# An encoder layer on one core: attention branch A's reciprocal row sums are transposed once and read back from DRAM spread over the channels, instead of being widened and transposed tile by tile

## The chip, the cores and the metric

The kernel runs on one core of a Trainium2 chip. The metric is the device time of one execution in microseconds (us); less is better. Before the change three runs gave 1674.7, 1675.51 and 1675.98 us.

Names of the engines in what follows: PE is TensorE (matmuls and transposes), DVE is VectorE, ACT is ScalarE, POOL is GpSimd, and SP is SyncE, which here only issues DMAs. Each engine works through its own instructions in order.

## The reference

One encoder layer (width 1024) is applied to two inputs: 1024 positions (the sample) and 256 positions (the prompt). The kernel works on both as one list of 1280 rows, 10 tiles of 128. Everything is float32.

```
h = rmsnorm(x, g_mix);  z = h @ w_in          # queries, keys, values of A and B, and gate logits
o_a = banded_attention(8 heads of 64, window 128, with a sink per head)     # branch A
o_b = dilated_mixture(3 groups x 4 heads of 64)                             # branch B
merged = sigmoid(gate_a) * (o_a @ w_branch_a) + sigmoid(gate_b) * (o_b @ w_branch_b)
x = x + merged @ w_out
y = rmsnorm(x + square(relu(rmsnorm(x, g_mlp) @ w_up)) @ w_down, g_final)
```

What matters here is the end of branch A's attention. For each position and head the kernel has the sum of the unnormalized values and the denominator; the output is their quotient:

```
denom = sum(p) + exp(sink - m)
o = (p @ v) / denom
```

## The kernel before, in words

A float32 product is made of three matmuls of a reduced type (fp32r): each operand is split into a high and a low part (`hi`, `lo`), high on ACT (a copy), low on DVE (a subtraction). `mm3` (line 188) emits them.

The stages that matter follow each other on PE. First comes **the attention of branch A** (lines 1430 to 1459): four units (two heads each) times ten tiles, with the last gate logits of `logits` (line 1223, the "fill") woven in between, 4 matmuls of 512 columns or 8 of 256 at a step. `exponential` (line 1177) leaves each row's sum in `l_a`, 128 positions x (8 heads x 10 tiles). `values_of` (line 1198) writes the unnormalized output, transposed, so that its partitions are the channels of two heads (64 each) and its columns the positions, to DRAM (`scr_o`). `sums_a` (line 1215) adds the sink's part and takes the reciprocal of `l_a`, in place, on DVE.

Then comes **the gate stage** (lines 1469 to 1540), 48 jobs. A job is one block of positions (512, 512 or 256), one branch, and one 128-wide group of the 1024 columns. A `b` job has 6 matmuls, an `a` job 12; the order is 8 `b` jobs of block 0, then 4 `a` jobs of block 0, then the same for blocks 1 and 2, then the remaining `a` jobs. Each job's result is multiplied on DVE by its gate `sg` (lines 1535 to 1538), which SP loads from DRAM six jobs ahead (`load_gate`, line 1473) and ACT turns into a sigmoid three jobs ahead (`open_gate`, line 1483). A job's matmuls go to one of the three PSUM banks of tag `mm`.

Beside those jobs the `a` operand is made (`side`, line 1504): `load_o` (line 1387) reads two tiles of `scr_o` back; `widen` (line 1394) copies, on POOL, `l_a`'s reciprocals of two tiles out to `wl`, 128 positions x (8 heads x 64), each value 64 times; `turn_a` (line 1400) transposes the four 128x128 squares of a tile's `wl` on PE into a PSUM bank, multiplies `o` with it on DVE (line 1409), and makes the high part on ACT (line 1415); `low_a` (line 1417) makes the low part on DVE. The first `a` job needs all of this for tiles 0 to 3. It also needs its weights, which `prepare` (line 224) splits: ACT at line 231, DVE at line 235.

What sets the order: up to `last.close()` (line 1503) the program's order is kept on every engine as written (`manual_schedule`). From there to line 1635, which holds the whole gate stage, a planner orders each engine's instructions, by the program's order as priority and by its own estimate of when each one's inputs and buffers are there. On the chip each engine then keeps that order, whether or not it has to wait. Tiles come from shared rings: `slot` hands out the 33 buffers of tag `m` (`sg`, `o`, `wl`, and the high and low parts), `wslot` the 10 of tag `w`.

Of the kernel before, what the change touches and what calls it, by code (L numbers as in the profile page):

```python
# [10 lines left out]
F32 = mybir.dt.float32  # L11
F32R = mybir.dt.float32r
AF = mybir.ActivationFunctionType
ALU = mybir.AluOpType

P = 128
# [3 lines left out]
T = NS + NP  # L20
NT = T // P
BLOCKS = ((0, 512), (512, 512), (1024, 256))
HD = 64
AH = 8
# [26 lines left out]
HALVES = (slice(0, HD), slice(HD, P))  # L51
# [46 lines left out]
def encoder_kernel(  # L98
# [5 lines left out]
    nc = tc.nc  # L104
# [16 lines left out]
    dram = ctx.enter_context(tc.tile_pool(name="dram", bufs=1, space=bass.MemoryType.DRAM))  # L121
# [5 lines left out]
    def slot(name, shape=(P, D), dt=F32):  # L127
        return slots.tile(list(shape), dt, name=name, tag="m", bufs=N_M)
# [7 lines left out]
    def bank(tag, name=None):  # L136
        return psum.tile([P, 512], F32, name=name or tag, tag=tag, bufs={"mm": 3, "sc": 2, "pt": 2, "pv": 1}[tag])
# [58 lines left out]
    def run(gen):  # L196
        for _ in gen:
            pass
# [47 lines left out]
    ident = const.tile([P, P], F32, name="ident")  # L246
# [4 lines left out]
    nsink = const.tile([P, AH], F32, name="nsink")  # L251
# [25 lines left out]
    scr_n = dram.tile([2, ROWS * P], F32, name="scr_n")  # L277
    scr_c = dram.tile([1, ROWS * P], F32, name="scr_c")
    scr_o = [dram.tile([P, 4, 2, P], F32, name=f"scr_o{t}") for t in range(0, NT, 2)]
    scr_x = [dram.tile([P, D], F32, name=f"scr_x{t}") for t in range(NT)]  # L280

    scr_u = [dram.tile([P, 7, 4, TH], F32, name=f"scr_u{g}") for g in range(FF // P // 8)]
# [383 lines left out]
    def load_h21():  # L666
        for i in range(2):
            h21[i] = slot("hhi", (P, 2, 512), F32R), slot("hlo", (P, 2, 512), F32R)
            for j in range(2):
                nc.sync.dma_start(h21[i][j].bitcast(F32), scr_h[i][:, j])  # L670
# [18 lines left out]
    with ExitStack() as pre:  # L689
# [200 lines left out]
        for t in range(2, NT):  # L890
# [13 lines left out]
            ps = bank("mm", "v")  # L904
# [20 lines left out]
        for t in (4, 5, 6, 7, 8, 9, 0, 1, 2, 3):  # L925
            ps = bank("mm", "v")
# [6 lines left out]
    if True:  # L933
# [188 lines left out]
        b, p = iter(()), parts0  # L1122
        att_b = iter(())
        for first, last, name in ((0, MIXED, "pairs"), (MIXED, len(PAIRS), "mixed")):
            with tc.tile_pool(name=name, bufs=1) as now[0]:
                if first:
                    att_b = attention_b(stage)
                for j in range(first, last):
# [4 lines left out]
                    b, p = pair(b, p, PAIRS[j], PAIRS[j + 1] if j + 1 < len(PAIRS) else None, hooks, tick, first)  # L1133
# [10 lines left out]
    if True:  # L1144
        att_pool = ExitStack()
        att = att_pool.enter_context(tc.tile_pool(name="att", bufs=3))
        nm_a, l_a = (att.tile([P, AH, NT], F32, name=x, tag=x, bufs=1) for x in ("nm_a", "l_a"))

        def a3(name, shape=(P, 2, 3 * P), n=3, dt=F32):
            return att.tile(list(shape), dt, name=name, tag=name, bufs=n)  # L1150
# [61 lines left out]
            nc.vector.tensor_copy(o, pv[:, : 2 * P].rearrange("p (i q) -> p i q", i=2))  # L1212
            nc.sync.dma_start(scr_o[t // 2][:, u], o)

        def sums_a():

            sinks = nsink.unsqueeze(2).to_broadcast([P, AH, NT])
            nc.vector.tensor_tensor(nm_a, nm_a, sinks, op=ALU.subtract)
            nc.scalar.activation(nm_a, nm_a, AF.Exp)
            nc.vector.tensor_tensor(l_a, l_a, nm_a, op=ALU.add)  # L1220
            nc.vector.reciprocal(l_a, l_a)

        def logits():

            for i, c in enumerate(PLAIN):
                hi, lo = weight(0)
                for t0, n in BLOCKS[::2] + BLOCKS[1:2]:
                    if i + 1 < len(PLAIN) and t0 == 0:
                        fetch()
                    ps = bank("mm")  # L1230
                    yield from mm3(ps[:, :n], [((hi[:, k, :], lo[:, k, :]), h_at(k, t0, n)) for k in range(KC)],
                                   4 if n == 512 else 8)
                    z = wslot("gs", (P, 512))
                    nc.scalar.activation(z[:, :n], ps[:, :n], AF.Copy)
                    nc.sync.dma_start(scr_g[c][:, t0 : t0 + n], z[:, :n])
                    if i + 1 < len(PLAIN) and t0 == NS:
                        prepare()
# [132 lines left out]
    if True:  # L1370
# [18 lines left out]
                rows_o[t] = slot("o", (P, 4, 2, P))  # L1389
                nc.sync.dma_start(rows_o[t], scr_o[t // 2])  # L1390

        wide_l = {}

        def widen(t):

            r = wide_l[t // 2] = slot("wl", (P, 2, AH, HD))
            for i in range(2):
                nc.gpsimd.tensor_copy(r[:, i], l_a[:, :, t + i].unsqueeze(2).to_broadcast([P, AH, HD]))

        def turn_a(t):  # L1400
            if t in (0, 4, 8):
                o_hi.block(t // 4)
                o_lo.block(t // 4)
            o = rows_o[t - t % 2][:, :, t % 2, :]
            ps = bank("pt")
            r = wide_l[t // 2][:, t % 2].rearrange("p h d -> p (h d)")
            for k in range(4):
                nc.tensor.transpose(ps[:, P * k : P * k + P], r[:, P * k : P * k + P], ident)
            nc.vector.tensor_tensor(o, o, ps.rearrange("p (k q) -> p k q", k=4), op=ALU.mult)
            per = o_hi.per(P * t)  # L1410
            parts = [(o_hi.at(k, P * t, P, per), o_lo.at(k, P * t, P, per), o[:, k : k + per, :])
                     for k in range(0, 4, per)]
            banks_t["a", t] = parts
            for hi, _, src in parts:
                nc.scalar.activation(hi, src, AF.Copy)

        def low_a(t):
            for hi, lo, src in banks_t.pop(("a", t)):
                nc.vector.tensor_tensor(lo, src, hi.bitcast(F32), op=ALU.subtract)

        load_h21()
        load_prompt(0, unit0[0])
# [2 lines left out]
        n = len(order)  # L1425
# [34 lines left out]
        prepare()  # L1460
        values_of(*order[n - 2])
        sums_a()
        run(merges)
        next(fill)
# [8 lines left out]
        def load_gate(i):  # L1473
            if i < len(jobs):
                x, b, c = jobs[i]
                t0, n = BLOCKS[b]
                if c % 2 == 0:
                    z = slot("sg", (P, 2, 512))
                sgs[i] = z[:, c % 2, :n] if c % 2 == 0 else sgs[i - 1, 0][:, 1, :n]
                sgs[i, 0] = z if c % 2 == 0 else None  # L1480
                nc.sync.dma_start(sgs[i], scr_g[c + KC * (x == "b")][:, t0 : t0 + n])

        def open_gate(i):
            if i < len(jobs):
                c = jobs[i][2] + KC * (jobs[i][0] == "b")
                nc.scalar.activation(sgs[i], sgs[i], AF.Sigmoid, bias=bg[:, c : c + 1])
# [5 lines left out]
        load_gate(3)  # L1492
        load_o(3)
        for i in range(4):
            if i < 2:
                widen(2 * i)
            if i < 3:
                open_gate(i)
            next(fill)
        run(fill)  # L1500
        load_gate(4)
        load_gate(5)
        last.close()
        side = {0: [(turn_a, 0)], 1: [(low_a, 0), (turn_a, 1)], 2: [(low_a, 1)],
                3: [(turn_a, 2), (widen, 4)], 4: [(low_a, 2), (turn_a, 3)], 5: [(low_a, 3)],
                6: [(high_b, 1)], 7: [(low_b, 1)],
                9: [(turn_a, 4), (widen, 6)], 10: [(low_a, 4), (turn_a, 5)], 11: [(low_a, 5)],
                13: [(turn_a, 6), (widen, 8)], 14: [(low_a, 6)], 15: [(turn_a, 7)], 16: [(low_a, 7)],
                17: [(high_b, 2)], 18: [(low_b, 2)],
                20: [(turn_a, 8)], 21: [(low_a, 8)], 22: [(turn_a, 9)], 23: [(low_a, 9)]}  # L1510
        for i, (x, b, c) in enumerate(jobs):
            t0, n = BLOCKS[b]
# [15 lines left out]
            ps = bank("mm")  # L1528
# [79 lines left out]
    with ExitStack() as pre:  # L1608
# [20 lines left out]
        for hh in range(2):  # L1629
# [17 lines left out]
            for t in range(NT):  # L1647
                m = parts.pop(t)
                ps = bank("mm")
# [393 lines left out]
```

## Time and profile before

| | before |
|---|---|
| runs shown, us | 1674.7, 1675.51, 1675.98 (median 1675.51) |
| span of the profiled execution, us | 1672.7 |
| median of the runs above that span, us | 2.8 |
| PE busy, us | 1661.8 (99%) |
| DVE / ACT / POOL busy, us | 951.1 / 714.3 / 494.3 |
| granted PE clock in the gate stage | 1.00 |
| HBM read / written, MB | 175.13 / 90.92 |

The span runs from the first to the last instruction that the profiler recorded. The times of the runs hold what lies around it; the page gives the profiled execution no other time of its own than the span. The two agree to within 2.8 us, 0.2%. The profile dates every instruction in us from the start of the span: the attention of A ends near 671, the fill near 681, and the gate stage reaches to about 770. A matmul's duration is modelled and overlaps the next one's; what a matmul takes of PE's time is the distance from its start to the next start.

### The profile page before, as it was taken

The page shows a single profiled execution, that of the slowest core. Times are in us where ns is not written, and L with a number is a line of the kernel's source. Part 1 is how long each engine was busy: PE and PEld are TensorE (multiplying, and loading weights), DVE is VectorE, ACT ScalarE, POOL GpSimd, SP SyncE. Part 2 cuts the span into 40 slices and gives each one's busy share as a digit, 9 for nine tenths or more (in the row PEclk, how much of TensorE's full clock was granted, in tenths as well). Part 3 has the DMA queues.
Part 4 walks back from the last instruction along what each step waited for, and adds up shares of the span by engine and source line. Part 5 has one row for each costly group of instructions (what it writes and reads, how often), then busy time and mean ns, then how long its engine had stood idle before and what let it go on. Part 6 is the DMA issues. An engine that isn't in the chain of part 4 may idle for free.

```text
span 1672.7 us, 24767 instructions
## 1 busy us (share of the span) xinstructions
PE 1661.8 (99%) x9256; PEld 1413.9 (85%) x9256; DVE 951.1 (57%) x1534; ACT 714.3 (43%) x1473; POOL 494.3 (30%) x372
## 2 busy tenths in 40 slices
PE   9999999999999999999999999999999999999998
PEld 7898888888888888888888888888888888888886
DVE  6732233455654565667278545445456775867665
ACT  6232323345654655654176333333334333333435
POOL 1212222111112352100100656455554250514240
PEclk9999999999999999999999999999999999999999
DMA  7416552666667794845121443343356934733333
GB/s 256 150 54 126 134 132 75 165 196 189 198 184 228 192 236 134 284 135 193 38 89 59 161 160 120 121 161 125 116 191 230 362 113 137 253 104 107 120 120 126
DMA packets 224176, 262.45 MB, mean 157 GB/s; under 512 B 29486, under 2 KB 153694, under 8 KB 224056
## 3 DMA queue, kind: packets, MB, share of 16 engines
q1 hardware_dynamic: 217000, 242.69, 45.4%
q0 software_dynamic: 6720, 17.65, 5.1%
q8 instruction: 73, 1.20, 0.3%
q10 hardware_dynamic: 336, 0.53, 0.1%
q14 instruction: 47, 0.39, 0.1%
HBM read 175.13 MB, written 90.92 MB: 159 GB/s over the span
## 4 chain that ended last, share of the span: by engine, by line
PE 96%; ACT 2%; DVE 1%; DMA 1%; issue 0%; SPq 0%; DVEq 0%; ACTq 0%
PE dn L345 22%; PE x L345 19%; PE mm L192 14%; PE z L345 10%; PE v L819 6%; PE y L345 5%; PE mm L345 5%; PE pv L345 3%; PE sc L345 3%; PE pt L1193 2%; PE pv L1209 2%; PE sc L553 1%; PE pv L600 1%; PE pt L586 1%; PE tr L336 1%; PE sc L1167 1%
## 5 line engine op out<-in xcount | busy, mean ns | idle before, releaser
L345 PE MATMUL dn<-dhi,ulo 128*128 128x512 f32 x448 | 174.3, 389 | 0.0
L345 PE MATMUL dn<-dlo,uhi 128*128 128x512 f32 x448 | 174.3, 389 | 0.0
L345 PE MATMUL dn<-dhi,uhi 128*128 128x512 f32 x448 | 174.3, 389 | 0.0
L345 PE MATMUL x<-chi,wlo 128*128 128x512 f32 x424 | 166.5, 393 | 0.0
L345 PE MATMUL x<-clo,whi 128*128 128x512 f32 x424 | 165.6, 390 | 0.0
L345 PE MATMUL x<-chi,whi 128*128 128x512 f32 x424 | 165.0, 389 | 0.0
L312 DVE TENSOR_TENSOR wlo<-ta,whi 128x1024 fp32r<-128x1024 f32 x30 | 56.3, 1876 | 174.0 <-ACT whi L310 174.0
L312 DVE TENSOR_TENSOR wlo<-raw,whi 128x1024 fp32r<-128x1024 f32 x60 | 89.6, 1494 | 103.1 <-ACT whi L310 98.2
L391 POOL TENSOR_TENSOR tb<-raw 128x512 f32<-128x512 f32 x25 | 32.3, 1290 | 363.7 <-DMA raw<-in_w_in_dram 111.8
L345 PEld LDWEIGHTS dn<-dhi,ulo 128*128 128x128 f32 x448 | 84.1, 188 | 17.6
L345 PEld LDWEIGHTS dn<-dhi,uhi 128*128 128x128 f32 x448 | 84.1, 188 | 17.4
L345 PEld LDWEIGHTS dn<-dlo,uhi 128*128 128x128 f32 x448 | 84.1, 188 | 17.4
L345 PEld LDWEIGHTS x<-chi,whi 128*128 128x128 f32 x424 | 79.6, 188 | 17.1
L345 PEld LDWEIGHTS x<-chi,wlo 128*128 128x128 f32 x424 | 79.8, 188 | 15.1
L345 PEld LDWEIGHTS x<-clo,whi 128*128 128x128 f32 x424 | 79.8, 188 | 14.6
L1735 POOL TENSOR_TENSOR t<-raw,t 128x1024 f32<-128x1024 f32 x16 | 46.4, 2924 | 149.2 <-DMA raw<-in_w_down_dram 149.2
L186 DVE TENSOR_TENSOR ulo<-uraw,uhi 128x1024 fp32r<-128x1024 f32 x56 | 86.1, 1558 | 4.4 <-ACT uhi L185 4.4
L1886 DVE TENSOR_TENSOR v<-v,dn 128x512 f32<-128x512 f32 x90 | 59.7, 683 | 42.3 <-PE dn L345 42.3
L186 DVE TENSOR_TENSOR dlo<-raw,dhi 128x1024 fp32r<-128x1024 f32 x32 | 50.1, 1590 | 46.3 <-ACT dhi L185 45.3
L1986 POOL TENSOR_TENSOR u<-u,u 128x640 f32<-128x640 f32 x16 | 25.1, 1569 | 173.3 <-ACT u L1904 173.3
L345 PE MATMUL dn<-dhi,up 128*128 128x512 f32 x224 | 73.5, 389 | 0.0
L345 PE MATMUL z<-chi,wlo 128*128 128x512 f32 x184 | 71.6, 389 | 0.0
(319 smaller groups left out, 4619.2 us busy)
## 6 DMA issues: line engine op xcount, KB each, us to landing
scr_u<-u SPq DMA_DIRECT2D x112, 320.0 KB, 2.6
uraw<-scr_u SPq DMA_DIRECT2D x56, 512.0 KB, 3.9
raw<-in_w_down_dram SPq DMA_DIRECT2D x36, 512.0 KB, 6.7
raw<-in_w_up_dram SPq DMA_DIRECT2D x32, 512.0 KB, 5.2
raw<-in_w_in_dram SPq DMA_DIRECT2D x25, 512.0 KB, 5.2
sg<-scr_g SPq DMA_DIRECT2D x32, 256.0 KB, 6.2
uraw<-scr_u SPq DMA_DIRECT2D x28, 256.0 KB, 4.5
qk<-scr_kb SPq DMA_DIRECT2D x48, 128.0 KB, 2.6
```

Source lines behind the costliest of these rows:

```text
L186: nc.vector.tensor_tensor(lo, src, hi.bitcast(F32), op=ALU.subtract)
L192: nc.tensor.matmul(ps, a, b, start=i == 0, stop=i == len(seq) - 1)
L312: nc.vector.tensor_tensor(lo, src, hi.bitcast(F32), op=ALU.subtract)
L336: nc.tensor.transpose(ps[:, P * i : P * (i + 1)], xn[t][:, P * k : P * (k + 1)], ident)
L345: nc.tensor.matmul(ps, a, b, start=first and i == 0, stop=last and i == len(seq) - 1, skip_group_check=True)
L391: (nc.vector if vector else nc.gpsimd).tensor_tensor(o, x, y, op=ALU.subtract)
L819: nc.tensor.matmul(ps[:, :n], a, b, start=k == 0 and j == 0, stop=k == KC - 1 and j == 2)
L1193: nc.tensor.transpose(ps[:, P * k : P * k + P], s[:, h, P * b : P * b + P], ident)
L1209: nc.tensor.matmul(pv[HALVES[h], P * i : P * i + P], src, pt[:, at + 2 * b + h, :], start=b == 0, stop=b == W // P - 1, skip_group_check=True)
L1735: nc.gpsimd.tensor_tensor(o, a, b, op=ALU.subtract)
L1886: nc.vector.tensor_tensor(v, v, ps, op=ALU.add)
L1986: nc.gpsimd.tensor_tensor(u[S1], u21, u22, op=ALU.add)
```

## The change

`sums_a` is only moved down in the file; it is called at the same place. `rows_a` is new: PE transposes `l_a` (128 positions x 80) once, into a PSUM bank of tag `mm`; DVE copies the 80 x 128 result to SBUF; a DMA from POOL's queue writes it to a new DRAM tensor `scr_l1`, 8 heads x 1280 positions. `widen` no longer copies on POOL: it reads `scr_l1` back with two DMAs from POOL's queue, one for each half of the partitions. For 64 partitions and four head pairs it reads the same 1 KB row (256 positions) of `scr_l1` 64 times, so that `wl` already has channels as partitions, 128 x (4 x 256), 512 KB in all. `turn_a` loses its four transposes and its bank of tag `pt`; DVE multiplies `o` by `wl` from SBUF.

The calls: before, `widen(0)` and `widen(2)` stood ahead of the first two of the last four single steps of the fill; now `rows_a()`, `widen(0)` and `widen(2)` stand behind the second of these steps. `widen(4)`, `widen(6)` and `widen(8)` are called where they were, in jobs 3, 9 and 13 of the gate stage.

```diff
+    scr_l1 = dram.tile([AH, T], F32, name="scr_l1")
...
-        wide_l = {}
-        def widen(t):
-            r = wide_l[t // 2] = slot("wl", (P, 2, AH, HD))
-            for i in range(2):
-                nc.gpsimd.tensor_copy(r[:, i], l_a[:, :, t + i].unsqueeze(2).to_broadcast([P, AH, HD]))
...
         def turn_a(t):
...
             o = rows_o[t - t % 2][:, :, t % 2, :]
-            ps = bank("pt")
-            r = wide_l[t // 2][:, t % 2].rearrange("p h d -> p (h d)")
-            for k in range(4):
-                nc.tensor.transpose(ps[:, P * k : P * k + P], r[:, P * k : P * k + P], ident)
-            nc.vector.tensor_tensor(o, o, ps.rearrange("p (k q) -> p k q", k=4), op=ALU.mult)
+            nc.vector.tensor_tensor(o, o, wide_l[t // 2][:, :, P * (t % 2) : P * (t % 2) + P], op=ALU.mult)
...
+        def rows_a():
+            ps, n = bank("mm", "tn"), AH * NT
+            nc.tensor.transpose(ps[:n, :P], l_a.rearrange("p h t -> p (h t)"), ident)
+            rows = a3("o", (P, 2, P), 3)[:n, 0, :]
+            nc.vector.tensor_copy(rows, ps[:n, :P])
+            a = scr_l1[:, :]
+            nc.gpsimd.dma_start(bass.AP(a.tensor, a.offset, [[P, n], [1, P]]), rows)
+
+        wide_l = {}
+
+        def widen(t):
+            r = wide_l[t // 2] = slot("wl", (P, 4, 2 * P))
+            a = scr_l1[:, :]
+            for h in range(2):
+                nc.gpsimd.dma_start(r[HALVES[h]], bass.AP(a.tensor, a.offset + T * h + P * t, [[0, HD], [2 * T, 4], [1, 2 * P]]))
...
         for i in range(4):
-            if i < 2:
-                widen(2 * i)
             if i < 3:
                 open_gate(i)
             next(fill)
+            if i == 1:
+                rows_a()
+                widen(0)
+                widen(2)
```

More of the change, by code (lines that the diff above doesn't have):

```diff
@@ L1213, in values_of @@
             nc.sync.dma_start(scr_o[t // 2][:, u], o)
[L1215 to L1221, printed above, removed]
         def logits():
@@ L1419, in low_a, with sums_a @@
                 nc.vector.tensor_tensor(lo, src, hi.bitcast(F32), op=ALU.subtract)
+        def sums_a():
+            sinks = nsink.unsqueeze(2).to_broadcast([P, AH, NT])
+            nc.vector.tensor_tensor(nm_a, nm_a, sinks, op=ALU.subtract)
+            nc.scalar.activation(nm_a, nm_a, AF.Exp)
+            nc.vector.tensor_tensor(l_a, l_a, nm_a, op=ALU.add)
+            nc.vector.reciprocal(l_a, l_a)
+        def rows_a():
[11 more added lines that the diff above has]
+                nc.gpsimd.dma_start(r[HALVES[h]], bass.AP(a.tensor, a.offset + T * h + P * t, [[0, HD], [2 * T, 4], [1, 2 * P]]))
         load_h21()
```

## The prediction

> **What bounds the kernel now.** I read the page first, then the waits of PE, the chain of waits and the windows of the stretch that the change touches, and last the rows of single instructions.
>
> ```profile
> span 1672.7 us, 24767 instructions
> PE 1661.8 (99%) x9256; PEld 1413.9 (85%) x9256; DVE 951.1 (57%) x1534; ACT 714.3 (43%) x1473; POOL 494.3 (30%) x372
> ```
>
> PE is busy 99% of the span at the full granted clock, so a PE instruction that goes is worth its time unless PE waits soon after for something that doesn't move. The answer for the tile `wl` and the chain of waits (start, length, what) say what goes and where such a wait stands:
>
> ```profile
> L1408 PE MATMUL pt<-ident,wl x40: 270/272/277, 680.7 to 724.4; 128*128 128x128 f32 x40
> L1398 POOL COPY wl<-l_a x10: 603/610/1639, 672.6 to 694.1; 128x512 f32<-128x512 f32 x10
> ```
> ```profile
> 680.85 0.44 PE pt L1408 x4
> 681.28 1.39 PE mm L192 x6
> ...
> 685.04 5.88 DMA sg<-scr_g
> ...
> 690.95 1.39 ACT sg L1486 x2
> 692.33 0.61 ACT ohi L1415 x2
> 692.95 0.96 ACT whi L231
> ...
> 694.03 1.20 DVE wlo L235
> ...
> 695.27 12.56 PE mm L192 x54
> 707.83 0.44 PE pt L1408 x4
> ...
> 724.23 0.44 PE pt L1408 x4
> ```
>
> A group of four transposes costs the path 0.44 us. From 707.83 to 724.23 the chain holds four such groups (16 transposes, tiles 6 to 9) with PE never out of work. The other 24 lie before 695.27, and there the chain leaves PE: from 685.04 it runs over a gate's load, two sigmoids, the high part of `o`, and the splitting of the first `a` weight, which PE's first `a` job needs. PE itself stood still at this place, the only such wait in the stage:
>
> ```profile
> PE mm L192 <- DVE wlo L235: 0.8, 1, 0.8
> ```
>
> The chain shows 1.03 us of it (from the end of the last transposes to 695.27); 0.8 is what the waits count. The load took 5.88 us because the DMA engines are full. In the windows the columns are PE, PEld, DVE, ACT and POOL busy, granted clock, DMA share and GB/s:
>
> ```profile
> 676.00:680.00 4.00, 4.00 (x20) 3.29 (x18) 0.00 (x0) 0.78 (x2) 0.92 (x2) 1.00 0.56 201
> 680.00:684.00 4.00, 4.00 (x23) 3.35 (x22) 1.54 (x3) 2.40 (x7) 1.17 (x2) 1.00 0.59 155
> 684.00:688.00 4.00, 4.00 (x24) 3.38 (x23) 3.63 (x8) 1.47 (x4) 0.00 (x0) 1.00 1.02 340
> 704.00:708.00 4.00, 4.00 (x21) 3.28 (x20) 2.87 (x6) 1.14 (x3) 0.00 (x0) 1.00 1.05 383
> ```
>
> **The change part by part.** *Transposes removed.* 40 go, 10 groups at 0.44 us, 4.4 us of PE. The four groups behind 695.27 are on the path and nothing late stands near them: 4 x 0.44 = 1.76 us gained. The six before it (2.64 us) bring PE sooner to the first `a` job, but that job's start is set by the chain 685.04 to 695.23, in which PE has no part. They are worth nothing as long as that chain stands, and 2.64 us if it moves forward as much.
>
> *The one transpose added.* It stands behind the second of the last four steps of the fill, that is after eight 256-column matmuls, at 673.29:
>
> ```profile
> 671.76 0.65 DVE L1221 RECIPROCAL l_a<-l_a 128x80 f32<-128x80 f32 x1
> 672.43 1.23 DVE L235 TENSOR_TENSOR wlo<-raw,whi 128x1024 fp32r<-128x1024 f32 x1
> 673.17 0.28 PE L192 MATMUL mm<-plo,whi 128*128 128x256 f32 x1
> 675.21 0.40 PE L192 MATMUL mm<-hhi,wlo 128*128 128x512 f32 x1
> 675.63 0.58 ACT L1234 ACTIVATE gs<-mm 128x512 f32<-128x512 f32 x1
> 680.98 1.17 POOL L1398 COPY wl<-l_a 128x512 f32<-128x512 f32 x2 [4.07 <-PE mm L192]
> 681.32 0.69 DVE L1409 TENSOR_TENSOR o<-o,pt 128x512 f32<-128x512 f32 x1 [7.66 <-PE pt L1408]
> ```
>
> The reciprocals are done at 672.41, so PE doesn't wait for them. The price is one transpose with the switch to it, between 0.11 us (a quarter of a group) and 0.44 us (a whole one). It falls before the wait at 695.27, which hides it; without that cover it costs these 0.1 to 0.4.
>
> *The way over DRAM.* The rows that are nearest, by tile or line (min/median/max in ns) and as DMA issues (KB each, us from issue to landing):
>
> ```profile
> L1259 DVE COPY cb<-tn x1: 424/424/424, 534.9 to 534.9; 120x256 f32<-120x256 f32 x1
> ```
> ```profile
> L452 POOL DMA_DIRECT2D bias<-wide x4: 712/716/740, 524.2 to 613.5; - x4
> ```
> ```profile
> scr_b<-o POOLq DMA_DIRECT2D x18, 64.0 KB, 2.5
> scr_n<-cb POOLq DMA_DIRECT2D x1, 48.0 KB, 5.9
> bias<-wide POOLq DMA_DIRECT2D x4, 256.0 KB, 4.4
> wide<-scr_l POOLq DMA_DIRECT2D x3, 512.0 KB, 9.8
> r<-scr_b SPq DMA_DIRECT2D x12, 256.0 KB, 6.4
> r<-scr_c SPq DMA_DIRECT2D x24, 128.0 KB, 6.4
> ```
>
> DVE is free at 672.43 + 1.23 = 673.66; the copy takes at most 0.42, so the dump (40 KB) is issued at 674.08. It lands 2.5 to 5.9 us later; I take 2.5, the single plain store, since the 5.9 is one of 13 stores issued back to back. The dump is thus there at 676.6. `widen(0)` issues two DMAs of 256 KB, 0.72 each on POOL; the second lands 4.4 us after its issue by the row of the same size and queue, at 676.6 + 0.72 + 4.4 = 681.7. The upper bound is the 9.8 us row, a broadcast out of DRAM like this one, but into DRAM and twice as large. I take 4.4, because the gate stage's own broadcast of 64 partitions (`r<-scr_c`) lands no later than the plain load beside it. `widen(2)` is two issues behind, at 683.2. Before, DVE's first product with `o` started at 681.32; now at 681.7. In DVE's queue behind it stand the second product and the first job's gate product, then done at 681.7 + 3 x 0.69 = 683.8. PE needs that only after three jobs of 1.39 us from 681, at 685.2, since the jobs turn over three banks. So the wait that is added is hidden, by 1.4 us.
>
> *POOL and DVE.* POOL loses ten copies and gets eleven issues; nothing else stands in its queue in the gate stage. DVE's product of 0.69 us reads SBUF instead of PSUM; the subtraction above does 1024 columns from SBUF in 1.23, that is 0.62 for 512. Neither is on the path: 0.
>
> *Bytes.* Each `widen` moves 512 KB, at the 340 to 383 GB/s of the full windows 1.37 to 1.54 us of all DMA engines, say 1.45. Three of them (tiles 0 to 5; `widen(4)` is issued as soon as a buffer is free, at 680.98 by the POOL row above) now fall between 677 and 684, ahead of the gate load of 685.04: 4.35 us. Free in these two windows were 4 x (0.44 + 0.41) = 3.4 us. So 0.9 us is left over and lands on that load, and with it on the start of the first `a` job: between 0 (all fits) and 4.35 us (nothing fits). The Trainium skill (DMA: Bandwidth & Descriptors, section Anatomy of one DMA — SWDGE (gpsimd) path) moves bytes at 436 GB/s behind a fixed 2.0 us: as an estimate by that page 1.2 us a widen, 3.6 in all, 0.2 left over, and the sum would be -1.6; the full windows here show 340 to 383 GB/s, and I go by them. The last two widens come when the path is PE's again and gates are loaded six jobs ahead: 0; if that cover were gone, 2.9 us.
>
> Sum: -1.76 + 0.9 = -0.9 us. That is against the profiled span, 1672.7, hence 1671.8; the runs lie 2.8 us above it, 1675.51 - 0.9 = 1674.6. PE's wait before the first `a` job would grow from 1.0 to 1.0 + 2.6 + 0.9 - 0.2 = 4.3 us.
>
> **The rivals.** *A, the chain moves too* (faster). With no transposes to wait for, DVE's products and ACT's high parts can be put ahead of the sigmoids, and ACT reaches the weight's splitting before the late gate. Then all ten groups count, less the added transpose: 4.4 - 0.2 = 4.2 us, 1671.3; if PE's own wait of 1.0 goes as well, 1670.3. For it: ACT's 0.61 us for `o` stands on the chain and is free to move. Against it: the sigmoids stand ahead of this weight in the program, and their load is held by full DMA engines, which get more to do.
>
> *B, the broadcast is slow* (slower). Reading one DRAM row 64 times costs what `wide<-scr_l` did, 9.8 us for each widen, one behind the other. With the dump at 5.9 us, `wl` of tiles 0 and 1 is there at 674.08 + 5.9 + 0.72 + 9.8 = 690.5, that of tiles 2 and 3 at 700.3; two products, the high and the low part (2 x 0.69 + 0.7 + 0.75) put the first `a` job at 703.1, 7.9 us late. Less 1.76, +6.1: 1681.6. It decides for slower by over 0.2% once the second `wl` lands after 697.6. Against it: the `r<-scr_c` row.
>
> ```profile
> L621 POOL DMA_DIRECT2D scr_b<-o x44: 538/540/579, 371.9 to 531.5; - x44
> ```
>
> These 44 issues from POOL, beside a working DVE, kept within 8%, and from 676 to 680 DVE did nothing at all; so B gets no more than its 0.2. The Trainium skill (SBUF — State Buffer, section SBUF: two separate sides) says against this change that a DMA issued from POOL can't get its descriptors written while DVE runs certain copies between SBUF tensors, and should go by SP or ACT. By that rule the dump and the four issues behind it could each wait for one DVE instruction (1.23 us in the row above), 6.2 us by the last: the sum would stay, but B would decide that much sooner. The rows here don't show it.
>
> *C, the bank.* The new transpose takes one of the three `mm` banks between the fill's last two blocks. If the block at 675.21 gets the bank that ACT empties only at 675.63 + 0.58 = 676.21, PE stands for 1.0 us, and what follows moves with it: -0.9 + 1.0 = +0.1, 1675.6, no change. For it: the bank that frees sooner, the transpose's, is the later one in the order of use.
>
> **How the numbers follow.** What a measurement of this kernel can tell from no change is about 0.2%, 3.4 us: below 1672.2 is faster, above 1678.9 slower. The likeliest, the gain of four groups less 0.9, has 0.45; its own range is 1672.7 to 1678, from a load not delayed and 1 us of the early groups kept, to 4.35 us of delay. C has 0.15, A 0.2, B 0.2. So faster 0.2, same 0.6, slower 0.2. The range of eight in ten reaches into both ends: 1670.8 to 1679.5.
>
> **What would show it.** Right: no L1408; the first product with `o` near 681.7; DMA share near full from 678 on; PE's wait ahead of the first `a` job about 4 us, on the same weight; that job near 696; 1.8 us less from there to the end of the stage. A would show the first `a` job near 693 and little waiting; B, DVE waiting on the landing of `wl` beyond 687 and PE on DVE's gate products; C, a wait of PE near 675 on ACT. The prediction is wrong if the six early groups are gained, or if a wait stands behind 700 that wasn't there.

## The result, and the profile after

The changed kernel takes 1683.69 us (median of 4 runs, 1681.0 to 1688.89) against 1675.37 for the kernel before in the same comparison: 8.3 us slower, ratio 1.0055 with a 95% interval of 1.0041 to 1.007. The prediction was 1674.6, in a range up to 1679.5.

The page of the kernel after begins so:

```profile
span 1687.1 us, 24682 instructions
PE 1664.0 (99%) x9217; PEld 1413.4 (84%) x9217; DVE 951.6 (56%) x1535; ACT 714.7 (42%) x1473; POOL 493.7 (29%) x373
```

The 39 transposes less are there (9256 matmuls before). The profiled execution is the slowest of the four, and 5.8 us of its excess lie in the first 30 us, where nothing was changed and PE's clock was low for a while. So times after are compared with times before from the same point on: the start of the last group of the attention's products, at 669.37 before and 675.18 after. From there to the first matmul of the stage behind the gates it is 100.06 us before and 108.70 after, 8.6 more; behind that the two run alike. All of the loss is in the gate stage.

PE's waits between 660 and 800 us (us in total, times, longest):

```profile
PE mm L192 <- DVE mT L1544: 10.0, 1, 10.0
PE mm L192 <- DVE wlo L235: 1.7, 2, 1.3
```

Before, there was one wait of 0.8 us on `wlo`. Now PE stands still for 10 us in one piece, and not where the prediction put its 4.3 us, ahead of the first `a` job, but among the `b` jobs: it waits for a gate product on DVE (line 1544), because its three banks are full. DVE's rows show what that product is queued behind, and POOL's rows when the DMAs were issued (start, length, engine, line; in brackets the idle time before and what ended it):

```profile
679.41 0.28 DVE L1415 COPY o<-tn 80x128 f32<-80x128 f32 x1
695.52 1.30 DVE L1390 TENSOR_TENSOR o<-o,wl 128x512 f32<-128x512 f32 x2 [15.82 <-DMA wl<-scr_l]
698.90 1.29 DVE L1390 TENSOR_TENSOR o<-o,wl 128x512 f32<-128x512 f32 x2 [2.09 <-issue]
700.12 0.68 DVE L1544 TENSOR_TENSOR mT<-mm,sg 128x512 f32<-128x512 f32 x1
```
```profile
679.99 0.60 POOL L1417 DMA_DIRECT2D scr_l<-o  x1 [26.57 <-DVE o L1415]
686.62 4.94 POOL L1426 DMA_DIRECT2D wl<-scr_l  x8 [6.03 <-DMA scr_l<-o]
705.81 1.23 POOL L1426 DMA_DIRECT2D wl<-scr_l  x2 [14.25 <-DVE olo L1400]
```

The planner put all four products of tiles 0 to 3 ahead of the first gate product. Behind the dump stand eight loads in a row, so four `widen`, not three. The answer for the tile `wl` and the row of the dump among the DMA issues (KB, us to landing):

```profile
L1426 POOL DMA_DIRECT2D wl<-scr_l x10: 617/626/649, 686.6 to 706.4; - x10
...
DMA to landing us min/median/max: 6.3/9.8/15.5
```
```profile
scr_l<-o POOLq DMA_DIRECT2D x1, 40.0 KB, 6.1
```

The windows of the stage (PE, PEld, DVE, ACT, POOL busy, granted clock, DMA share, GB/s):

```profile
680.00:684.00 4.00, 4.00 (x24) 3.51 (x23) 0.00 (x0) 1.93 (x3) 0.59 (x1) 1.00 0.93 319
684.00:688.00 4.00, 4.00 (x20) 3.30 (x19) 0.00 (x0) 2.20 (x4) 1.38 (x3) 1.00 0.38 83
...
692.00:696.00 4.00, 0.00 (x0) 0.00 (x0) 0.48 (x1) 0.00 (x0) 0.00 (x0) 0.77 1.05 265
696.00:700.00 4.00, 0.00 (x0) 0.00 (x0) 1.91 (x4) 1.97 (x5) 0.00 (x0) 0.50 1.03 242
700.00:704.00 4.00, 3.15 (x7) 2.49 (x8) 3.85 (x10) 1.96 (x4) 0.00 (x0) 0.50 1.05 260
```

Three things are to be seen. While the dump was on its way (684 to 688) the DMA engines had little to do (share 0.38): the free time that the prediction meant to fill went by unused. When the loads ran, the engines were full, but moved only 242 to 265 GB/s where the full windows of before move 340 to 387. And PE's clock fell to half during the stop and was still there when it began again.

How long the engines are full is told best by the timeline of the DMA in 40 slices of 1.5 us, before (670 to 730) and after (676 to 736, so that both begin at the same point of the work):

```profile
DMA  0598950399999999999999999750008648600798
GB/s 0 143 341 296 318 199 23 96 219 350 320 330 321 350 393 385 373 389 406 366 363 370 365 391 383 246 164 3 0 11 262 171 132 251 223 0 0 235 253 283
```
```profile
DMA  0699950659999999999999999999999999865073
GB/s 0 145 335 289 324 225 21 102 100 312 326 266 244 242 253 234 253 255 264 214 388 392 356 222 221 380 397 391 386 360 377 356 378 380 283 177 171 0 210 85
```

Before, 17 slices (25.5 us) without a break are full, from 682 on; after, 25 slices (37.5 us). In that stretch the gates' loads, the `o` loads and the weights of the `a` jobs already filled the DMA engines in the kernel before. The chain of waits of after runs over them:

```profile
688.32 12.07 DMA sg<-scr_g
...
700.40 14.25 DMA raw<-in_w_branch_a_dram
...
714.67 1.07 ACT whi L231
...
715.76 1.24 DVE wlo L235
...
717.04 5.06 PE mm L192 x21
```

The gate load takes 12.07 us and the weight load 14.25. The loads in the same places of SP's queue took 4.16 and 7.67 us in the kernel before, by the issues and landings in its trace.

### The profile page after: what moved, and what is told of

Read it like the earlier page. It is cut to its first block, busy times and chain, and to the rows that moved or that the text cites. A ratio compares the mean times of both kernels' runs of the same rounds, so it can differ in the third digit from the quotient of the medians.

```text
span 1687.1 us, 24682 instructions
## 1 busy us (share of the span) xinstructions
PE 1664.0 (99%) x9217; PEld 1413.4 (84%) x9217; DVE 951.6 (56%) x1535; ACT 714.7 (42%) x1473; POOL 493.7 (29%) x373
## 4 chain that ended last, share of the span: by engine, by line
PE 94%; DMA 2%; ACT 1%; DVE 1%; SPq 0%; issue 0%; ACTq 0%
PE dn L346 22%; PE x L346 19%; PE mm L192 13%; PE z L346 10%; PE v L820 6%; PE y L346 5%; PE mm L346 5%; PE pv L346 3%; PE sc L346 3%; PE pv L1210 2%; PE pt L1194 2%; PE sc L554 1%; PE pv L601 1%; PE pt L587 1%; DMA sg<-scr_g 1%; DMA raw<-in_w_branch_a_dram 1%
## 5 line engine op out<-in xcount | busy, mean ns | idle before, releaser
L346 PE MATMUL z<-clo,whi 128*128 128x512 f32 x184 | 71.7, 389 | 0.0
```

The source lines that it names most:

```text
L346: nc.tensor.matmul(ps, a, b, start=first and i == 0, stop=last and i == len(seq) - 1, skip_group_check=True)
```

## The experiments

Two theories stood at first. **Trip**: the price is the wait of DVE's products for `wl`, whose landing is late and which stand ahead of the gate products. **Traffic**: the price is the time that the new loads take from DMA engines that are already full; whichever engine waits is then only the place where it shows. (The expectations call the first "lateness" or T, the second "DMA traffic" or S.) Below, "before" is the median of the kernel before, run beside each experiment (1674.5 to 1675.4). Where a ratio stands, it compares round by round with the kernel before, so it can differ a little from the quotient of the medians; its 95% interval is in brackets. PE's waits are those from 660 to 800 us.

**1. Is it the one row that is read 64 times?**

```diff
-            a = scr_l1[:, :]
+            a = scr_qa[3][:, :, :, :]
...
-                nc.gpsimd.dma_start(r[HALVES[h]], bass.AP(a.tensor, a.offset + T * h + P * t, [[0, HD], [2 * T, 4], [1, 2 * P]]))
+                nc.gpsimd.dma_start(r[HALVES[h]], bass.AP(a.tensor, a.offset + P * t, [[T, HD], [HD * T, 4], [1, 2 * P]]))
```

> The changed kernel, but each of the 64 partitions reads a DRAM row of its own (queries of branch A, already there) instead of all reading the same one; as many bytes, the same issues, and still behind the dump. The values multiplied in are therefore not the reciprocals. Theory 'one row read 64 times is slow': the DMA engines go back from about 240 to about 365 KB/us while these loads run, a load lands in about 5 us instead of 8 to 11, PE's stop shrinks from 10 us to 4 or 5, time about 1678. Theory 'the round trip is late whatever the rows are': loads land as before, PE stops 9 to 10 us, time 1683 to 1684.

1683.36 us, ratio 1.0045 (1.0028 to 1.0061). PE's stop is 10.0 again, the median landing 9.6, and the rate stays low:

```profile
692.00:696.00 4.00, 0.48 (x1) 0.48 (x2) 2.43 (x5) 1.00 (x3) 0.00 (x0) 0.50 1.05 236
```

The reason that rival B gave for a slow broadcast falls: other rows cost the same.

**2. How much is the way, how much the transposes?** First with tiles 0 to 3 done as before, and only 4 to 9 over DRAM (1 MB of loads ahead of the first `a` job instead of 2 MB):

```diff
+            if t < 4:
+                ps = bank("pt")
+                r = wide_l[t // 2][:, t % 2].rearrange("p h d -> p (h d)")
...
...
+            if i < 2:
+                widen_old(2 * i)
...
-                widen(0)
-                widen(2)
```

> Tiles 0 to 3 by the old way (POOL copies, PE transposes), tiles 4 to 9 over DRAM. Theory 'lateness': nothing waits for the trip any more, the stop of 10 us is gone, and what is left is the gain of six groups: 1672.7 (all six) to 1673.6 (the four behind the first a job). Theory 'DMA traffic': the three loads that are left still hold up the gates and the weight of the first a jobs, PE waits 1 to 3 us more than before there, time 1675 to 1678.

1679.34 us, 1.0023 (1.0013 to 1.0032). Then with no factors at all:

```diff
-            nc.vector.tensor_tensor(o, o, wide_l[t // 2][:, :, P * (t % 2) : P * (t % 2) + P], op=ALU.mult)
+            nc.vector.tensor_tensor(o, o, o, op=ALU.mult)
...
-            if i == 1:
-                rows_a()
-                widen(0)
-                widen(2)
```

> The changed kernel without the dump and the loads, and with o multiplied by itself instead of by the reciprocals: what the change could bring if the trip cost nothing. If the first a job is held by the gates as the prediction had it, only four groups count: 1673.6. If the early groups count as well: 1671.0; if PE's wait of 1.0 before the first a job goes too: 1670.

1673.4 us, 0.9991 (0.9981 to 1.0): 2.0 less than before by the medians, 1.5 by the ratio, whose interval reaches to no gain at all. PE's waits of the two:

```profile
PE mm L192 <- DVE mT L1557: 4.8, 1, 4.8
```
```profile
PE mm L192 <- DVE mT L1540: 3.2, 1, 3.2
```

The second row is without any trip: PE, sooner at this place, waits for a chain of gate load, sigmoid, high and low part. It begins like the one that the prediction named, but it ends at a gate product among the `b` jobs. In the first row tiles 0 to 3 wait for nothing from DRAM, and yet the gate stage is late; a gate load ahead of the first `a` job landed at 691.3 instead of 687.1. That speaks for traffic.

**3. The trip 15 us sooner.**

```diff
-            nc.tensor.transpose(ps[:n, :P], l_a.rearrange("p h t -> p (h t)"), ident)
+            nc.tensor.transpose(ps[:n, :P], l_b[:, :n], ident)
...
+            if j == n - 6:
+                rows_a()
+                widen(0)
+                widen(2)
```

> The changed kernel with the transpose, the dump and the first two loads some 15 us earlier, in the last rounds of the attention; it turns branch B's sums (already there) instead of A's, so the values multiplied in are not the reciprocals. As many bytes, as many issues. Theory 'lateness': the stop is gone, 1671 to 1674. Theory 'DMA traffic': the bytes cost what they cost wherever they are, 1677 or more, with PE waiting for gates or weights.

1678.67 us, 3.3 above before; by the ratio, 1.001 (1.0001 to 1.002), it is 1.7. Its dump, and a window in which its loads had the DMA engines nearly to themselves:

```profile
scr_l<-o POOLq DMA_DIRECT2D x1, 40.0 KB, 2.3
```
```profile
660.00:662.00 2.00, 2.00 (x25) 1.83 (x22) 1.75 (x3) 0.93 (x3) 0.00 (x0) 1.00 1.04 217
```

Here the dump lands in 2.3 us, about as the prediction took it; in the kernel after it took 6.1. The load on the engines alone doesn't explain that: between issue and landing their mean share was 0.79 here and 0.64 there. The packets tell where the time went. Here the first of the dump's 16 began 1.2 us after the issue and all were done by 655.8. There the first began 2.9 us after it, and the last one at 685.50, when the other 15 had been written by 684.2. What they queued behind isn't shown. The loads run at 217 GB/s even alone, with the engines' time used up (share 1.04). What stayed of PE's waits:

```profile
PE mm L192 <- ACT gs L1227: 3.0, 1, 3.0
PE mm L192 <- DVE mT L1544: 2.9, 1, 2.9
```

The first looks like rival C, but isn't: ACT came late to empty the bank, because a sigmoid ahead of that copy had waited 7.3 us for its gate load (to 684.42). The second ends behind another gate load, for which ACT waited 5.2 us. Both are late gates, as Traffic has it; but with the trip earlier the price is much smaller, which fits Trip as well.

**4. The form of the loads.** The same bytes, issues and pieces, but each load goes to all 128 partitions:

```diff
-            a = scr_l1[:, :]
+            a = scr_qb[0][0][:, :]
...
-                nc.gpsimd.dma_start(r[HALVES[h]], bass.AP(a.tensor, a.offset + T * h + P * t, [[0, HD], [2 * T, 4], [1, 2 * P]]))
+                nc.gpsimd.dma_start(r[:, 2 * h : 2 * h + 2], bass.AP(a.tensor, a.offset + 516 * h + 8 * t, [[T, P], [258, 2], [1, 2 * P]]))
```

> The same ten 256 KB loads of wl at the same places behind the same dump, in the same 1 KB pieces, but each load writes all 128 partitions (two of the four head pairs) where the kernel after writes 64 partitions (all four head pairs). The rows read are others and different on each partition, so wl holds wrong values. Theory P (a load into half of the partitions gets only about half of the DMA system's rate, whatever it reads): while the loads run, 340 to 380 KB/us are moved where after shows 235 to 265; the loads of tiles 0 to 3 land about 4 to 6 us after issue (after: 9.8 median), PE's stop before the first a job shrinks from 10 to 3 to 6 us, time 1676 to 1680. Rival Q (it is the number of bytes, or POOL's queue, or the 1 KB pieces): rate 210 to 265 KB/us as before, PE's stop 9 to 10 us, time 1682 to 1685.

1678.9 us, 1.0028 (1.0018 to 1.0039): 4.4 above before instead of 8.3. The window and the waits:

```profile
688.00:692.00 4.00, 0.00 (x0) 0.00 (x0) 2.48 (x4) 2.06 (x5) 0.00 (x0) 0.77 1.04 366
```
```profile
PE mm L192 <- DVE mT L1544: 7.6, 1, 7.6
```

366 GB/s at the same share, so the rate of theory P was met; the stop shrank less than P expected, though the time fell as it said. The Trainium skill (SBUF — State Buffer, section Door 1: The DMA port swizzle) has the rule: partitions 0 to 63 reach only 8 of SBUF's 16 DMA ports, good for some 218 GB/s, and two transfers to the two halves don't add up. The 217 GB/s of the run above agree with it.

**5. Only tiles 6 to 9 over DRAM** (0.5 MB ahead of the first `a` job; the edit is that of 2 with `t < 6`).

> Tiles 0 to 5 get their factors as in the kernel before (POOL copies, transposes), tiles 6 to 9 over DRAM. Then the two loads of widen(6) are the only ones that can be issued before the first a job, and they can't be needed before 700. Theory T (the slower time comes from the loads being too late and too many ahead of the first a job): with 0.5 MB there instead of 2 MB, the gate load ahead of the first a job is late by 0 to 2 us, PE waits 1 to 3 us, and four groups of transposes (1.8 us) are saved behind it: 1673.5 to 1676. Rival S (the trip costs something wherever it is, by its traffic alone): as with the first four tiles old, 1679 to 1680.

1675.09 us against 1674.52, 1.0002 (0.9993 to 1.0011); PE's only wait is 0.9 on `wlo`. Four groups of transposes saved, and half a megabyte paid: no difference.

**6. More time for the trip.** The jobs in another order, b0, b1, a0, a1, b2, a2, with the new way and, as its measure, with the old:

```diff
-        jobs = [(x, b, c) for b in range(3) for x in "ba" for c in range(KC if x == "b" else 4)]
+        jobs = [(x, b, c) for x, b in ("b0", "b1", "a0", "a1", "b2", "a2") for b in (int(b),) for c in range(KC if x == "b" else 4)]
...
```

> The kernel after with the gate stage's jobs in the order b0, b1, a0, a1, b2, a2 (eight b jobs more ahead of the first a job, 11 us of PE's work); nothing else is changed. Theory T: the trip has its time, wl of tiles 0 to 3 is there before the first a job, PE's stop is 0 to 2 us, and most of the 40 transposes are gained: 1670 to 1674. Rival S (the traffic costs the gate loads as much wherever it falls): the gates of the b jobs come late instead, PE waits 5 to 10 us in all: 1679 to 1685.

> The kernel before with the same other order of jobs as the run beside it (b0, b1, a0, a1, b2, a2): the measure for that run. The wait of about 1 us before the first a job goes; the transposes stay: 1674 to 1676 by every theory. The difference to the run beside it is then the worth of the trip where it has time: by T 1 to 4 us in its favour, by S 4 us or more against it.

1682.75 (1.0049, 1.0037 to 1.0062) and 1676.48 (1.001, 1.0001 to 1.0019): the new way costs 6.3 us where it should have had 11 us more, against 8.3. But the planner had again put the products ahead of all gate products on DVE (the first at 688.88, the first gate product at 693.90), so the slack was not used, and the run did not decide.

**7. The order kept by hand.** That made the next theory, D: it is the planner's order on DVE. The program's order was kept through the first eight jobs, with the products behind the eighth gate product; beside it the kernel before, kept likewise; and the order of 6, kept through sixteen jobs.

```diff
-        last.close()
...
+        behind = {7: [(turn_a, 0), (turn_a, 1), (low_a, 0), (low_a, 1), (turn_a, 2), (turn_a, 3), (low_a, 2), (low_a, 3)]}
...
+            if i == 8:
+                last.close()
...
```

> The kernel after, its loads and their places unchanged, but through the first eight jobs of the gate stage every engine keeps the order of the program, and the products, high parts and low parts of tiles 0 to 3 are written behind the gate product of the eighth job. Theory D (half of the lost time comes from the order: the planner put the products of tiles 0 to 3 ahead of the gate products on DVE, so PE's three banks fill up while DVE waits for a landing): PE's stop of 10 us on a gate product is gone; PE waits 3 to 5 us ahead of the first a job, for the low part of o; time 1674 to 1678. Rival S (the loads hold the DMA engines, so the gate loads are late in any order): PE waits 8 us or more in all, 1681 to 1684.

> The measure for the run beside it: the kernel before with the program's order kept through the first eight jobs, its products of tiles 0 to 3 behind the gate products of jobs 0 to 5. Nothing waits for DRAM here; by every theory 1673 to 1677.

> As the kernel after with the jobs in the order b0, b1, a0, a1, b2, a2 (which took 1682.75 under the planner), but with the program's order kept through the first sixteen jobs, and the products of tiles 0 to 3 behind the gate products of jobs 9 to 14. Theory D: now the trip really has 11 us more; PE's stop of 8.5 us goes, at most 1 to 2 us of waits stay, and the transposes are gained: 1671 to 1675. Rival S: gate loads late because of the traffic, PE waits 5 us or more in all: 1678 to 1683.

1695.87, 1677.61 and 1685.3 us. D fell in both places: it wanted 1674 to 1678 and 1671 to 1675. PE's and ACT's longest waits in the first of them, and PE's in the last:

```profile
PE mm L192 <- ACT ohi L1396: 20.8, 1, 20.8
```
```profile
ACT sg L1493 <- DMA sg<-scr_g: 24.9, 10, 8.4
```
```profile
PE mm L192 <- DVE mT L1544: 11.0, 2, 10.7
```

In neither run does PE wait for a gate product that stands behind `wl`, and the gates themselves are late: in the first, ACT waits ten times, 24.9 us in all, for gate loads. There the last of the early loads landed at 702.5, and DVE's first product with it is 8.5 us later, so here the trip held nothing up:

```profile
710.99 1.28 DVE L1390 TENSOR_TENSOR o<-o,wl 128x512 f32<-128x512 f32 x2
```

**8. The traffic alone.** The kernel before, whole, with eight loads of 256 KB more, in the form of the kernel after, that nothing reads; and the same into all partitions:

```diff
         run(fill)
+        for t in range(4):
+            r, y = slot("idle", (P, 4, 2 * P)), scr_g[15][:, :]
+            for h in range(2):
+                nc.gpsimd.dma_start(r[HALVES[h]], bass.AP(y.tensor, y.offset + T * h + P * 8, [[0, HD], [2 * T, 4], [1, 2 * P]]))
```

> The kernel before, whole, with eight loads added from POOL's queue at about the place where the kernel after issues the loads of tiles 0 to 7: the same 2 MB in the same form (64 partitions each, one row for all), out of the gate logits' DRAM tensor, into buffers that nothing reads. No step of the work waits for them. Theory S (the traffic alone is the price): the gate loads land late, PE waits 8 us or more in all, 1681 to 1686. Rival T (the price is the way over DRAM: products that wait for the factors): nothing waits, 1674.5 to 1676.

> The same 2 MB of loads that nothing reads, each into all 128 partitions instead of 64. By theory P (loads into half of the partitions run at about half the rate, and hold up the others) the extra DMA time falls from about 9.5 to 5.5 us: 3 to 5 us less than the run beside it, 1677 to 1681. Without P (bytes alone count) the two take the same time, within 1 us.

1692.39 (1.012, 1.0099 to 1.0142) and 1681.91 us (1.0042, 1.0029 to 1.0055). Traffic that nobody waits for makes the kernel slower, and the two forms are 10 us apart. But the planner had also moved weight loads ahead of gate loads on SP, three in the first and one in the second, and in the first one of them took 17.46 us. So both were repeated on the kept order of 7, where SP's queue is the same load for load:

> The kernel before with the program's order kept through the first eight jobs (that took 1677.6, 1.0021 of before), plus the eight loads of 64 partitions each that nothing reads. The planner cannot move SP's or DVE's work ahead because of them this time: SP's queue is the same, load for load. Theory S (traffic alone): gate loads and weight loads land late, PE waits 10 us or more in all, 1687 to 1697. If the 17 us of the earlier run with such loads came from the planner's other order (two more weight loads ahead of the gates): 1678 to 1682.

> The same with the loads into all 128 partitions. Theory P (the half-partition form holds the DMA engines about twice as long): 5 us or more below the run beside it, 1680 to 1686, and 340 to 380 KB/us while the loads run, against 200 to 260. Without P: the same time as the run beside it, within 2 us.

1687.1 (1.0077, 1.0063 to 1.009) and 1683.28 us (1.005, 1.0038 to 1.0063). The kept kernel before was 3.1 us above its own before; these are 11.8 and 8.0 above theirs. So 2 MB of loads that nothing reads cost 8.7 us in the half-partition form and 4.9 in the full one. The difference of 3.8 is less than the 5 that was expected. By the ratios the prices are 9.4 and 4.9; the intervals leave some 2 to 3 us of room on each. A window of each, and the DMA timeline in slices of 1.5 us from 670 on for the kept kernel before, with half-partition loads, and with full ones:

```profile
692.00:696.00 4.00, 3.20 (x16) 2.67 (x16) 1.94 (x4) 0.72 (x1) 0.24 (x1) 1.00 1.06 237
```
```profile
692.00:696.00 4.00, 2.71 (x17) 2.10 (x15) 1.28 (x2) 1.34 (x3) 1.25 (x3) 1.00 1.04 347
```
```profile
DMA  0598962047999999999999999912300375890039
```
```profile
DMA  0589972049999999999999999999999991500057
```
```profile
DMA  0589780246999999999999999999970212019749
```

16, 24 and 19 full slices: the loads lengthen the full stretch by 12 and by 4.5 us, and the kernel by 8.7 and 4.9.

**9. The loads behind the full stretch.** As in 2, tiles 0 to 3 the old way, but a small copy on POOL ties the loads of tiles 4 to 9 to the results of later jobs:

```diff
             r = wide_l[t // 2] = slot("wl", (P, 4, 2 * P))
+            nc.gpsimd.tensor_copy(r[:, 0, :1], mT.at(*late[t])[:, :1])
...
+        behind = {10: [(widen, 4)], 11: [(widen, 6)], 17: [(widen, 8)]}
...
```

> Tiles 0 to 3 as in the kernel before, tiles 4 to 9 over DRAM; against the earlier run of that kind (1679.34) only the loads are later: a small copy on POOL ties those of tiles 4 and 5, 6 and 7, 8 and 9 to the results of jobs 10, 11 and 17, and the products of tiles 4 to 7 are written two to six jobs later. The loads then fall behind 702, into the stretch in which the DMA engines are nearly idle (share 0.2 to 0.6 behind 708 in the kernel before). Theory S (the DMA engines are the bound from 684 to 708, and a load costs PE time only there): the gate loads come as in the kernel before, PE waits 0.5 to 2 us in all, the transposes of tiles 6 to 9 (1.8 us) are gained: 1672.5 to 1675. Rival T (a wait on the trip itself, wherever it is): 1677 to 1680.

1679.27 us, 1.0025 (1.0014 to 1.0035): no better than with the loads early. PE's waits and the DVE row of the first late product:

```profile
PE mm L192 <- DVE wlo L235: 2.0, 1, 2.0
PE mm L192 <- DVE mT L1559: 1.9, 2, 1.0
PE mm L192 <- ACT ohi L1403: 1.0, 1, 1.0
```
```profile
713.75 0.69 DVE L1397 TENSOR_TENSOR o<-o,wl 128x512 f32<-128x512 f32 x1 [2.92 <-DMA wl<-scr_l]
```

The first wait has no load of `wl` near it (the first is issued at 706.71); the order had changed. The next two are the trip itself: issued at 706.71, while the engines were still full, landed at 713.7, with the product ahead of gate products. Inconclusive: it shows that a late load is not free either, not what one in an idle stretch would cost.

**10. The half clock.**

```diff
         run(fill)
+        idle, w = bank("pv", "idle"), w_bs[0][0]
+        for _ in range(44):
+            nc.tensor.matmul(idle, w[:, 0, :P], w[:, 1, :], start=True, stop=True, skip_group_check=True)
```

> The kernel after with 44 matmuls of 512 columns between the fill and the first job, whose result nothing reads (10 us of PE's work, about as long as PE stands still in the kernel after). Theory H (standing still costs PE its clock, about 2 us of half speed behind the stop): the granted clock stays 1.00 through the stretch, the stop is 0 to 1 us, and the time is 1681 to 1682.5. Rival (the halved clock has another cause than the stop, or costs nothing): clock 0.5 there as well, or time as that of the kernel after, 1683 to 1685.

1691.98 us, 1.0104 (1.009 to 1.0118). The 10 us of work did not fill the stop: it came as much later and was as long, and the clock is at 0.50 again from 700 to 708. So the run could not part the price of the clock from that of the stop. It tells more about the two theories:

```profile
PE mm L192 <- DVE mT L1547: 10.7, 1, 10.7
```
```profile
693.53 1.29 DVE L1390 TENSOR_TENSOR o<-o,wl 128x512 f32<-128x512 f32 x2 [2.14 <-issue]
703.75 1.23 DVE L235 TENSOR_TENSOR wlo<-raw,whi 128x1024 fp32r<-128x1024 f32 x1 [8.93 <-issue]
704.89 0.68 DVE L1547 TENSOR_TENSOR mT<-mm,sg 128x512 f32<-128x512 f32 x1
```

All four products with `wl` were done at 694.8, and only then, at 694.95, did PE's stop begin. DVE's queue now held a weight's low part ahead of the first gate product. Its high part came late from ACT, at 702.62, behind four sigmoids that had each waited for a gate load. The trip had its 10 us, and the stop stayed.

## Why the prediction was wrong, point by point

What each dose of loads cost, from the runs above (difference of the medians to the kernel before, run beside it). The doses also differ in the groups of transposes that are gone: 10 in the first row, 4 with 0.5 MB, 6 with 1 MB and 10 with 2 MB.

| loads ahead of the first `a` job | us |
|---|---|
| none, transposes gone (2) | -2.0 |
| 0.5 MB, half partitions (5) | +0.6 |
| 1 MB, half partitions (2) | +3.9 |
| 2 MB, half partitions, other rows (1) | +8.0 |
| 2 MB, half partitions: the change | +8.3 |
| 2 MB, all partitions (4) | +4.4 |

-2.0 for the transposes and +8.7 for 2 MB of traffic (8) make +6.7 of the measured +8.3; with all partitions, -2.0 + 4.9 = +2.9 of +4.4. The 1.6 and 1.5 that are left are within the intervals. They may belong to the trip's own waits and to the last `widen`; the runs don't show it. The sum also takes a price from the kept order of 7 over to another order, which is argued and not measured.

- *Transposes removed*: right in size. 1.76 was predicted, with nothing for the six early groups; without the trip the gain is 2.0 (1.5 by the ratio). That is all ten groups, 4.4 us, less 2.4 us more of waiting (3.2 instead of 0.8) for a chain that begins with a gate load, as the prediction's does.
- *The one transpose added*: right here. No wait of PE near it, so rival C didn't happen.
- *The way over DRAM*: the issue of the dump was right, 674.08 against 679.99 - 5.8 = 674.2. "I take 2.5, the single plain store" failed: 6.1 us, above the upper bound of 5.9. The DMA share was 0.93 from 680 to 684, but by experiment 3 the share alone doesn't tell a slow store from a fast one, so the reason stays open. The 4.4 for a load failed too: 9.8. That row is of loads into 128 partitions. The `r<-scr_c` row that was set against rival B was misread: it is of branch B's merge (579 to 639), not of the gate stage, and it moves 128 KB into 64 partitions in the 6.4 us in which the plain load beside it moves 256. The sign of the slow form stood there. The first product came at 695.52 - 5.8 = 689.7 instead of 681.7, so "hidden, by 1.4 us" was wrong. It was also wrong on the order: the products of all four tiles, not of two, went ahead of the first gate product.
- *Bytes*: this is the step that decided. "Three of them ... 4.35 us. Free in these two windows were ... 3.4 us. So 0.9 us is left over." There were four, for `widen(6)` was issued at once as well. They ran at 217 GB/s by themselves and held the whole at 242 to 265, not at 340 to 383. The free time was gone when the dump had landed (83 GB/s from 684 to 688). Left over were 8.7 us, by the run with the traffic alone on the kept order; the upper bound of 4.35 supposed the full rate and three loads.
- "The last two widens ... 0": wrong for one, as `widen(6)` belonged to the early four; for `widen(8)`, issued at 705.81, PE's 1.7 us on `wlo` behind a weight load of 14.25 us fit, but no run tests it.
- *Rivals*: B came nearest, 1681.6, with its landing of 9.8 us. Its reason, the row read 64 times, is refuted (1), and its place, the late `wl` in DVE's queue, is where PE's wait shows but not what it costs: with that queue freed the kernel was slower still (7), and with those products done in time the stop stayed (10). That its number came near is luck. A did not happen.
- What would show it: DMA share near full, as said, but from 689.5, not 678 (684 with the shift); PE's wait on gate products, which was given as B's sign.

The granted clock adds to the stop. PE stood from 690.84 to 700.86, and its first matmuls came every 0.43 us instead of 0.23 until 704.4; for 8 matmuls that is some 1.6 us, an estimate from these rows. PE's own time then adds up, as an estimate: 10.0 for the stop, 0.9 more on `wlo`, 1.6 for the clock, 0.1 to 0.4 for the added transpose, less 4.4 for ten groups, make 8.2 to 8.5 of the 8.6 us lost.

## What to carry to other kernels

Before work is moved from a busy engine to DMA, look for the stretches in which the DMA engines are full already: there much of the time added to them becomes the kernel's, whichever engine is seen waiting (here 8.7 us for a full stretch 12 us longer, and 4.9 for 4.5). Cost a load by its form, not only by its bytes: with the same bytes the windows moved 237 GB/s in the 64-partition form and 347 in the 128-partition one. And test a suspected transfer by adding it to the unchanged kernel with nobody waiting for it, with the order held fixed; that told traffic from latency here when three other experiments had not.

## What the runs showed of the hardware

- Loads of 256 KB into 64 partitions, all reading one row, ran at some 217 GB/s with nothing beside them and the DMA engines' share at 1.04. Among other loads the windows show 237 to 265, and 236 where each partition reads a row of its own; with loads into 128 partitions 347 to 366.
- A 40 KB store from POOL's queue landed in 2.3 us in one run and in 6.1 in another, and the mean DMA share meanwhile was higher in the first (0.79 against 0.64).
- PE's granted clock falls to 0.50 within about 4 us of a stop (0.77 in the window that begins 1.2 us after it) and is back some 3.6 us after work begins. The Trainium skill (TensorE: Matmul & The Clock Gate, section Part 1: The HAM clock gate) states half clock after an idle window of about 3.4 us and full clock after as long a busy one; these rows agree.
